# Hybrid decoder step on one core: store queue, T's DRAM tile, a gate buffer and a filler's order in the mixer

## The chip, the cores and the metric

The kernel runs on one core of a Trainium2 chip. The metric is the device time of one execution in microseconds (us). A core has a matrix engine (PE, TensorE), three engines for elementwise work (DVE, ACT and POOL), and a sequencer without arithmetic (SP). SP, ACT and POOL also issue DMAs, each from its own queue and in program order: an instruction that waits holds back everything behind it on its engine.

## The reference

One layer of a decoder trunk for a prompt of 1024 tokens and 8 samples of 4 tokens: a gated feed-forward block, a mixer, and a second feed-forward block, each with a conditioned norm and a residual. The mixer has two branches that share an input and an output projection:

```
xb, gb, pr = h @ w_in                       # RG-LRU input, RG-LRU gate, RWKV rows
# RG-LRU: convolution of 4 taps, two gates, a linear recurrence, then the output gate
y_lru  = linear_scan(a, b, h0) * gelu(gb)
# RWKV-7, a head: state S [value, key], a token at a time
S = S * w_t + (S @ a_t) b_t^T + v_t k_t^T ;  y_t = S @ r_t
y_rwkv = (group_norm(y) + bonus) * g
out = concat(y_lru, y_rwkv) @ w_out
```

## The kernel before, in words

The program goes feed-forward, mixer, feed-forward. A float32 product is done as three matmuls on rounded parts (lines 61 to 63). The order of the instructions on each engine is settled when the program is built: a scheduler with a timeline of its own sorts what the code emits, and the code's generators say what may be mixed.

The mixer (about 940 to 1465 us) has two stages that matter here.

**Preparation.** For each of four pairs of heads there are steps for the projections, for token-major rows, and for the inverse T of the triangular matrix of each chunk of 64 tokens. `prep_v` turns three matrices into token-major rows: PE transposes a block into PSUM (`ptr`), ACT copies it to a buffer `kbv` (two buffers; blocks 0 to 3 share one, 4 to 7 the next, and the samples' block 8 is small), and DMAs store it in DRAM: six stores of 128 KB to `dC` after block 3 and six after block 7, and one of 48 KB to `dKs` after block 8. Between these steps stand those of the RG-LRU: convolution input (`lru_x`), gates and scan (`lru_g`), and output gate (`lru_e`: a gelu on ACT of the projection, written to a buffer called "D", then a product on DVE). T's blocks are written by `inverse` and `merge` into columns of `dC` and read back by `merge` (`iX`).

**Chain.** `chain` runs over 16 chunks. `load(c)` fetches the rows of a chunk from `dC` into `ch` (64 rows for each of two halves) and `X2`, two chunks ahead, from ACT's queue. Then a chunk is a sequence that goes back and forth: matmuls `pw` from `ch`, ACT copies them to `W`, matmuls `pu` multiply W by T, ACT and DVE copy them to `X2`, matmuls `pd` update the state, DVE adds (`St`, `ch` of the next chunk, lines 956 and 960). The output of two chunks goes through a group norm (`yc`, `gva`) and a transpose `ptY`. While this sequence waits for other engines, PE runs a filler, a generator that yields a step at a time: the samples' recurrence (`sample_rwkv`), the second half of the RG-LRU (`lru(2, 4)`), then the output projection w_out (`po`). In `sample_rwkv` the output rows are gathered by 8 DMAs of 8 KB into `y2`; what follows (`gated`) has DVE instructions that write `late` (lines 1003 and 1009).

Weights come in blocks `wr` of 512 KB by DMAs from SP's queue, one buffer, and ACT and DVE split each into two parts (`wh`, `wl`, lines 46 and 47). DMAs that SP and ACT issue share eight semaphores in turn, so an issue also waits until the DMA before it on the same semaphore has landed.

Of the kernel before, what the change touches and what calls it, by code (L numbers as in the profile page):

```python
# [8 lines left out]
F32 = mybir.dt.float32  # L9
# [5 lines left out]
D, NP, NB, TS = 1024, 1024, 8, 4  # L15
# [14 lines left out]
CL = 64  # L30
# [8 lines left out]
def trunk(tc, a):  # L39
    nc = tc.nc  # L40
    es = ExitStack()
    const = es.enter_context(tc.tile_pool(name="const", bufs=1, reuse_waits="tile"))
    PL_, m = {"wn": T}, {}
# [472 lines left out]
    dram = es.enter_context(tc.tile_pool(name="dram", bufs=1, space=bass.MemoryType.DRAM))  # L516


    RW = 2304
    dC = [dram.tile([NP, RW], F32, name=f"dc{h}") for h in range(2)]  # L520
    MN = (256, 0)
    OV = (0, 2048)
    O2, OT, OG = 1024, 1536, 1792
    dKs = dram.tile([2, 2, 32, 2, 192], F32, name="dks")
    dM = dram.tile([4, NC, 128, 64], F32, name="dm")
    dGs = dram.tile([2, 2, 32, 2, 128], F32, name="dgs")
# [245 lines left out]
    def prep_v(hp_, kt, bt, Pp, Ps, rk, bv):  # L772
        D_ = nc.gpsimd.dma_start
        v_ = shifted(8 + hp_, 16 + hp_)
        for ci, (c, n) in enumerate(CH):
            ps = Q([128, n], "pbo")
            nc.tensor.matmul(ps, rk, bv[:, c:c + n], start=True, stop=True)
            nc.vector.tensor_tensor(bv[:, c:c + n], ps, v_[:, c:c + n], op=ALU.mult)
        for par in range(2):
            D_(dBV[hp_ % 2, :, hp_ // 2, par], bv[64 * par:64 * par + 64])  # L780

        for s in range(9):
            n = 128 if s < 8 else 32
            pt = Q([128, 3, 128], "ptr")
            for j, src in enumerate((kt, bt, v_)):
                nc.tensor.transpose(pt[0:n, j, :], src[:, 128 * s:128 * s + n], ident)
            if s % 4 == 0:
                kb = PL_['sm_'].tile([128, 4, 2, 3, 64], F32, tag="kbv", name="kbv")
            nc.scalar.activation(kb[0:n, s % 4].rearrange("p a j v -> p j a v"), pt[0:n].rearrange("p j (a v) -> p j a v", a=2), AF.Copy)
            if s == 8:  # L790
                nc.scalar.dma_start(dKs[:, hp_ % 2, :, hp_ // 2].rearrange("a t f -> t a f"), kb[0:32, 0].rearrange("p a j v -> p a (j v)"))
            elif s % 4 == 3:
                for par in range(2):
                    o2 = O2 + 64 * (4 * par + hp_)
                    for j, h, off in ((0, 1 - par, MN[1 - par] + o2), (1, par, MN[par] + o2), (2, 1 - par, OV[1 - par] + 64 * hp_)):
                        nc.scalar.dma_start(dC[h][128 * (s - 3):128 * (s + 1), off:off + 64].rearrange("(b r) f -> r b f", r=128), kb[:, :, par, j])

    def trow(par, g, s0, t0):
        off = MN[par] + OT + 64 * g + t0
        return dC[par][:, off:off + 32].rearrange("(c s) t -> c s t", s=CL)[:, s0:s0 + 32]  # L800

# [94 lines left out]
    def chain(fill):  # L898
# [2 lines left out]

        def load(c):

            ch = PL_['rg'].tile([128, 2560], F32, tag="ch", name="ch")
            X2 = PL_['rg'].tile([128, 8, 64], F32, tag="X2", name="X2")
            for h in range(2):
                r = slice(64 * h, 64 * h + 64)
                nc.scalar.dma_start(ch[r, 256 * h:256 * h + RW], dC[h][CL * c:CL * c + CL])
                nc.scalar.dma_start(X2[r, 4 - 4 * h:8 - 4 * h].rearrange("p g v -> p (g v)"), dC[h][CL * c:CL * c + CL, OV[h]:OV[h] + 256])
            x1 = lambda par: ch[:, 0:256].rearrange("p (g v) -> p g v", g=4) if par else ch[:, 2304:2560].rearrange("p (g v) -> p g v", g=4)  # L910
            v4 = lambda o, n: ch[:, 256 + o:256 + o + n].rearrange("p (g t) -> p g t", t=64)
            return x1, X2, ch[:, 256:1280].rearrange("p (h j t) -> p h j t", h=8, j=2), v4(O2, 512), v4(OT, 256), v4(OG, 256)

        late, wait, FN = None, 0, CFG["fn"]

# [119 lines left out]
    def sample_rwkv(late):  # L1035
# [73 lines left out]
        for g2 in range(2):  # L1109
            es_ = tp.rearrange("p (j b v) -> p j b v", j=2, b=NB)  # L1110
            for j in range(2):
                src = kb[:, g2, 128:192] if j == 0 else U[:, g2]
                nc.vector.tensor_tensor(es_[:, j], src.unsqueeze(1).to_broadcast([128, NB, 64]), bm, op=ALU.mult)
            yield
            for l in range(2):
                update(g2, l, es_)
                yield
            nc.sync.dma_start(a["s_wkv"][:, 2 * g2:2 * g2 + 2], S0[g2])
            if g2 == 0:
                pt = MM([128, 128], "ptS")  # L1120
                nc.tensor.transpose(pt, yc[:, 0:2].rearrange("p a b -> p (a b)"), ident)
                ys = o([128, 128], F32, "ys")
                nc.scalar.activation(ys, pt, AF.Copy)
                y2 = o([128, 4, 32], F32, "y2")
                for h2_ in range(2):
                    for g1 in range(2):
                        for par in range(2):
                            q = 32 * (2 * par + g1)
                            nc.gpsimd.dma_start(y2[64 * g1:64 * g1 + 64, 2 * h2_ + par], ys[64 * h2_:64 * h2_ + 64, q:q + 32])
        sx.close()  # L1130
        yield
        gated(NP, 32, lambda j: y2[:, j].unsqueeze(1), o, "mm")
        yield

# [15 lines left out]
    def LR(s, n=T):  # L1150
        return LRT[0][:, LRT[1][s]:LRT[1][s] + n]
# [47 lines left out]
        nc.vector.tensor_copy(m["hO"][:, f, 0:1], gx[:, NP - 1:NP])  # L1199
        nc.vector.tensor_copy(m["hO"][:, f, 1:9].unsqueeze(2), smp(gx[:, NP:T])[:, :, 3:4])  # L1200

    def lru_e(f):
        h, ge = LR("C"), LR("D")
        for p in half_proj(4 + f):
            if p:
                ci, c, n, ps = p
                nc.scalar.activation(ge[:, c:c + n], ps, AF.Gelu_apprx_tanh)
                if f == 3:
                    nc.vector.tensor_tensor(h[:, c:c + n], h[:, c:c + n], ge[:, c:c + n], op=ALU.mult)
            yield  # L1210
        if f < 3:
            nc.vector.tensor_tensor(h, h, ge, op=ALU.mult)
            nc.gpsimd.dma_start(dY[f], h)

    def lru(f0, f1):
        yield from lru_x(f0)
        lru_conv(f0)
        for f in range(f0, f1):
            if f < f1 - 1:
                yield from lru_x(f + 1)  # L1220
            yield from lru_g(f)
            if f < f1 - 1:
                lru_conv(f + 1)
            yield from lru_e(f)

    def w_load(half, og):
        return [weight(a["w_out"][4 * half + 2 * j:4 * half + 2 * j + 2, :, 512 * og:512 * og + 512].rearrange("k p o -> p k o")) for j in range(2)]
# [352 lines left out]
    with ExitStack() as ph:  # L1580
# [28 lines left out]
        def filler():  # L1609
            s_, l_ = sample_rwkv(late), lru(CFG["order"].count("X"), 4)  # L1610
            next(s_)
            yield

            for used in range(CFG["pre"]):
                next(l_)
                yield
            used = CFG["pre"]
            for i, _ in enumerate(s_):
                yield
                for _ in range(CFG["mix"] if i >= CFG["st"] else 0):  # L1620
                    if used < 12:
                        used += 1
                        next(l_)
                        yield
            yield from l_
            wo = w_out()
            next(wo)
            to_y()
            yield from wo
# [125 lines left out]
```

## Time and profile before

| | before |
|---|---|
| median of 3 runs | 2238.94 us (2236.42 to 2241.89) |
| the profiled execution | 2240.2 us |
| its span, first to last instruction | 2238.4 us |
| mean granted PE clock | 0.972 |
| PE busy | 2113.9 us, 94% |
| DVE busy | 1409.3 us, 63% |
| ACT busy | 734.1 us, 33% |

The span is what the profile's clock of microseconds runs over; 1.8 us of the execution lie outside it. Busy time counts what an engine computes; waits on DMAs, and the issuing of DMAs, are not counted. The granted clock is PE's, 1.00 at 2.4 GHz and 0.50 at 1.2 GHz.

### The profile page before, as it was taken

To read this page: it belongs to the slowest core of one execution; us is meant where nothing else is said; L and a number is where in the kernel's file an instruction comes from. 1 tells how busy PE (TensorE), PEld (TensorE's weight loads), DVE (VectorE), ACT (ScalarE), POOL (GpSimd) and SP (SyncE) were. 2 spreads that over 40 slices of the span, in tenths; PEclk is the share of its full clock that TensorE was granted. 3 is DMA by queue.
4 is the path that set the end of the run, shared out by engine and by line. 5 is a ranking of instruction groups with operands and counts; after the bars stand their busy time and mean duration, and the time that the engine had idled before them with its cause. 6 is when DMAs were issued, how large, how long until landed. Compare 5 with 4: busy or idle time off the path is not lost.

```text
span 2238.4 us, 41844 instructions
## 1 busy us (share of the span) xinstructions
PE 2113.9 (94%) x17209; PEld 2000.5 (89%) x17209; DVE 1409.3 (63%) x2954; ACT 734.1 (33%) x1283; POOL 212.2 (9%) x314
## 2 busy tenths in 40 slices
PE   6899999999999999999887889979999999999997
PEld 4899999999999988888886668878999999999997
DVE  5755555565956566674844676578666666585655
ACT  5533232323312144343333251246333333331213
POOL 0000000000000041214220100100000000100004
PEclk9999999999999999999898999989999999999998
DMA  6244444443723121446476756441222222262312
GB/s 249 86 147 145 141 152 138 138 146 110 234 84 103 51 99 42 97 106 150 112 161 157 184 149 152 146 145 57 73 82 82 75 75 86 92 216 87 100 44 78
DMA packets 145662, 266.80 MB, mean 119 GB/s; under 512 B 75504, under 2 KB 90048, under 8 KB 143424
## 3 DMA queue, kind: packets, MB, share of 16 engines
q1 hardware_dynamic: 76672, 165.51, 23.5%
q0 software_dynamic: 19312, 63.18, 9.0%
q10 hardware_dynamic: 49488, 35.45, 7.0%
q8 instruction: 135, 2.21, 0.4%
q14 instruction: 55, 0.45, 0.1%
HBM read 200.20 MB, written 63.82 MB: 118 GB/s over the span
## 4 chain that ended last, share of the span: by engine, by line
PE 74%; DVE 9%; DMA 5%; issue 4%; ACT 4%; ACTq 1%; POOL 1%; DVEq 0%; POOLq 0%
PE pd L61 7%; PE pd L62 7%; PE pd L63 7%; PE pX L61 4%; PE pZ L61 4%; PE pX L62 3%; PE pZ L63 3%; PE pX L63 3%; PE pW L61 3%; PE pW L63 3%; PE pW L62 3%; PE pZ L62 3%; PE pY L63 2%; PE pY L61 2%; PE pY L62 2%
## 5 line engine op out<-in xcount | busy, mean ns | idle before, releaser
L61 PE MATMUL pd<-fl,wh 128*128 128x384 f32 (+1 forms) x1056 | 340.6, 325 | 3.2 <-DVE fl L47 2.6
L63 PE MATMUL pd<-fh,wh 128*128 128x384 f32 (+1 forms) x1056 | 341.6, 324 | 0.0
L62 PE MATMUL pd<-fh,wl 128*128 128x384 f32 (+1 forms) x1056 | 341.5, 324 | 0.0
L46 ACT ACTIVATE wh<-wr 128x512 fp32r<-128x512 f32 (+1 forms) x254 | 192.3, 761 | 249.9 <-PE pZ L63 71.7
L47 DVE TENSOR_TENSOR wl<-wr,wh 128x512 fp32r<-128x512 f32 (+1 forms) x254 | 215.1, 851 | 87.5 <-ACT wh L46 82.1
L61 PEld LDWEIGHTS pd<-fl,wh 128*128 128x128 f32 x1056 | 198.5, 189 | 4.9 <-ACT wh L46 2.7
L62 PEld LDWEIGHTS pd<-fh,wl 128*128 128x128 f32 x1056 | 199.7, 189 | 0.0
L63 PEld LDWEIGHTS pd<-fh,wh 128*128 128x128 f32 x1056 | 199.4, 189 | 0.0
L61 PE MATMUL pW<-t,wh 128*128 128x266 f32 (+1 forms) x640 | 182.6, 285 | 0.0
L63 PE MATMUL pW<-t,wh 128*128 128x266 f32 (+1 forms) x640 | 182.3, 285 | 0.0
L62 PE MATMUL pW<-t,wl 128*128 128x266 f32 (+1 forms) x640 | 182.2, 285 | 0.0
L463 DVE SCALAR_TENSOR_TENSOR x<-pd,g3c,x 128x384 f32<-128x384 f32 (+1 forms) x192 | 107.1, 569 | 82.6 <-PE pd L63 82.6
L463 DVE SCALAR_TENSOR_TENSOR x<-pd,g1c,x 128x384 f32<-128x384 f32 (+1 forms) x192 | 107.8, 568 | 76.8 <-PE pd L63 76.6
L344 POOL DMA_DIRECT2D dh<-hf x88 | 48.0, 546 | 976.0 <-DVE hf L425 793.8
L419 ACT ACTIVATE e<-e,bt 128x262 f32<-128x262 f32 x80 | 41.3, 516 | 293.4 <-DVE bt L418 273.8
L46 ACT ACTIVATE fh<-wr 128x1056 fp32r<-128x1056 f32 x44 | 47.6, 1082 | 246.5 <-PE pd L63 195.9
L62 PEld LDWEIGHTS pW<-t,wl 128*128 128x128 f32 x640 | 120.8, 189 | 0.0
L61 PEld LDWEIGHTS pW<-t,wh 128*128 128x128 f32 x640 | 120.5, 188 | 0.0
L63 PEld LDWEIGHTS pW<-t,wh 128*128 128x128 f32 x640 | 120.5, 188 | 0.0
L47 DVE TENSOR_TENSOR wl<-s,wh 128x512 fp32r<-128x512 f32 x120 | 82.7, 690 | 58.5 <-ACT wh L46 58.5
L416 DVE TENSOR_TENSOR e<-pZ,e 128x266 f32<-128x266 f32 x80 | 34.5, 431 | 104.3 <-PE pZ L63 104.1
L46 ACT ACTIVATE wh<-s 128x512 fp32r<-128x512 f32 x120 | 75.4, 629 | 68.4 <-PE pW L63 31.4
(496 smaller groups left out, 5908.5 us busy)
## 6 DMA issues: line engine op xcount, KB each, us to landing
wa<-in_w_ada SPq DMA_DIRECT2D x72, 512.0 KB, 4.0
dh<-hf POOLq DMA_DIRECT2D x88, 264.0 KB, 2.3
wr<-dh SPq DMA_DIRECT2D x44, 528.0 KB, 4.3
wr<-in_ffn_w_gate SPq DMA_DIRECT2D x44, 512.0 KB, 3.5
wr<-in_ffn_w_up SPq DMA_DIRECT2D x44, 512.0 KB, 3.5
wr<-in_ffn_w_down SPq DMA_DIRECT2D x44, 512.0 KB, 3.9
ch<-dc ACTq DMA_DIRECT2D x32, 576.0 KB, 7.2
wr<-in_w_in SPq DMA_DIRECT2D x22, 512.0 KB, 4.0
```

Source lines behind the costliest of these rows:

```text
L46: nc.scalar.activation(hi, raw, AF.Copy)
L47: nc.vector.tensor_tensor(lo, raw, hi.bitcast(F32), op=ALU.subtract)
L61: nc.tensor.matmul(ps, wh, xl, start=(first and i == 0), stop=False, **kw)
L62: nc.tensor.matmul(ps, wl, xh, start=False, stop=False, **kw)
L63: nc.tensor.matmul(ps, wh, xh, start=False, stop=(last and i == n - 1), **kw)
L344: nc.gpsimd.dma_start(self.dH[m][:, 528 * p:528 * p + 528], hf)
L416: tt(g2, pz, u, op=ALU.add)
L419: nc.scalar.activation(g2[:, 0:n], g2[:, 0:n], AF.Silu, bias=bt[:, 0:1])
L463: nc.vector.scalar_tensor_tensor(x[:, ob, c:c + np_], ps[:, 0:np_], g[:, ob, 0:1], x[:, ob, c:c + np_], op0=ALU.mult, op1=ALU.add)
```

## The change

Five edits, all in the mixer:

1. The stores of `prep_v` are issued from SP's queue and not from ACT's, and block 8 comes first and not last.
2. T has DRAM tiles of its own, `dTT[0]` and `dTT[1]` (256 columns); the rows of `dC` shrink from 2304 to 2048 columns. `load(c)` has two more DMAs of 64 KB a chunk (`tt`), issued from ACT's queue.
3. Of the 8 DMAs that gather `y2`, four are issued from SP's queue; all eight were on POOL's.
4. `lru_e` writes the gelu of the last feature block of each half to buffer "A", of the others to "D" as before.
5. The filler leaves `sample_rwkv` at the gather for eight steps of the RG-LRU, and then does the samples' gated output.

```diff
-    RW = 2304
+    RW = 2048
     dC = [dram.tile([NP, RW], F32, name=f"dc{h}") for h in range(2)]
...
-    OV = (0, 2048)
-    O2, OT, OG = 1024, 1536, 1792
+    OV = (0, 1792)
+    O2, OG = 1024, 1536
+    dTT = [dram.tile([NP, 256], F32, name=f"dtt{h}") for h in range(2)]
...
-        for s in range(9):
+        for s in (8, *range(8)):
...
-                nc.scalar.dma_start(dKs[:, hp_ % 2, :, hp_ // 2].rearrange("a t f -> t a f"), kb[0:32, 0].rearrange("p a j v -> p a (j v)"))
+                nc.sync.dma_start(dKs[:, hp_ % 2, :, hp_ // 2].rearrange("a t f -> t a f"), kb[0:32, 0].rearrange("p a j v -> p a (j v)"))
...
-                        nc.scalar.dma_start(dC[h][128 * (s - 3):128 * (s + 1), off:off + 64].rearrange("(b r) f -> r b f", r=128), kb[:, :, par, j])
+                        nc.sync.dma_start(dC[h][128 * (s - 3):128 * (s + 1), off:off + 64].rearrange("(b r) f -> r b f", r=128), kb[:, :, par, j])
...
     def trow(par, g, s0, t0):
-        off = MN[par] + OT + 64 * g + t0
-        return dC[par][:, off:off + 32].rearrange("(c s) t -> c s t", s=CL)[:, s0:s0 + 32]
+        off = 64 * g + t0
+        return dTT[par][:, off:off + 32].rearrange("(c s) t -> c s t", s=CL)[:, s0:s0 + 32]
...
                 nc.scalar.dma_start(ch[r, 256 * h:256 * h + RW], dC[h][CL * c:CL * c + CL])
+                nc.scalar.dma_start(tt[r].rearrange("p g t -> p (g t)"), dTT[h][CL * c:CL * c + CL])
...
-                            nc.gpsimd.dma_start(y2[64 * g1:64 * g1 + 64, 2 * h2_ + par], ys[64 * h2_:64 * h2_ + 64, q:q + 32])
+                            (nc.gpsimd, nc.sync)[g1].dma_start(y2[64 * g1:64 * g1 + 64, 2 * h2_ + par], ys[64 * h2_:64 * h2_ + 64, q:q + 32])
         sx.close()
-        yield
+        yield "y2"
...
-    def lru_e(f):
-        h, ge = LR("C"), LR("D")
+    def lru_e(f, at="A"):
+        h, ge = LR("C"), LR(at)
...
-            yield from lru_e(f)
+            yield from lru_e(f, "D" if f < f1 - 1 else "A")
...
-            for i, _ in enumerate(s_):
+            for i, at in enumerate(s_):
                 yield
+                if at:
+                    break
...
+            for _ in range(8):
+                next(l_)
+                yield
+            for _ in s_:
+                yield
             yield from l_
```

The scheduler sorts the instructions anew, so their order shows more than the diff. The first place is ACT in the third `prep_v`, before:

```order
L789 ACTIVATE kbv<-ptr 128x3x2x64 x3
L796 DMA dc_82<-kbv 128x4x64
L796 DMA dc_81<-kbv 128x4x64
L796 DMA dc_82<-kbv 128x4x64
L796 DMA dc_81<-kbv 128x4x64
L796 DMA dc_82<-kbv 128x4x64
L796 DMA dc_81<-kbv 128x4x64
L789 ACTIVATE kbv<-ptr 32x3x2x64
L1207 ACTIVATE lr<-pj 128x384
L1207 ACTIVATE lr<-pj 128x288
```

and the same place of the change (`L1207` is `L1210` there):

```order
L790 ACTIVATE kbv<-ptr 32x3x2x64
L790 ACTIVATE kbv<-ptr 128x3x2x64
L1210 ACT_TABLE_LOAD
L1210 ACTIVATE lr<-pj 128x384
L790 ACTIVATE kbv<-ptr 128x3x2x64 x7
L1210 ACTIVATE lr<-pj 128x384
L1210 ACTIVATE lr<-pj 128x288
```

No DMA stands between the copies any more; the twelve stores stand on SP, between two loads of `wr`.

The second place is ACT where the chain begins. Before, the loads of chunks 0 and 1 stand in two groups:

```order
L909 DMA X_12739<-dc_81 64x256
L909 DMA X_12739<-dc_82 64x256
L909 DMA X_12747<-dc_81 64x256
L909 DMA X_12747<-dc_82 64x256
L869 ACTIVATE iX<-pa 32x512 x2
L615 ACTIVATE x<-pj 128x384
L908 DMA ch<-dc_81 64x2304 x2
L908 DMA ch<-dc_82 64x2304 x2
```

In the change eight loads stand ahead of the last copies `iX` of `merge`, and those of T come after the first `W` (rows of the change from the last of the eight on):

```order
L912 DMA X_12753<-dc_82 64x256
L870 ACTIVATE iX<-pa 32x512 x2
L616 ACTIVATE x<-pj 128x384 x2
L618 ACTIVATE x<-pj 128x256
L619 ACTIVATE x<-pj 128x8x4
L46 ACTIVATE wh<-wr 128x1024
L1176 ACTIVATE x<-x,vec 128x1024
L1176 ACTIVATE x<-x,vec 128x32
L942 ACTIVATE W<-pw 128x256
L911 DMA tt<-dtt_83 64x256 x2
L911 DMA tt<-dtt_84 64x256 x2
L947 ACTIVATE X_12742<-pu 64x256
```

The loads of `ch` no longer stand behind `merge`, and those of T stand behind `W` of chunk 0.

The third place is PE in the last chunk. Before, rows of w_out stand between its steps, for instance around `pu` (52 `po` in all between `pw` and `ptY`):

```order
L63 MATMUL po<-h1hy,wh 128x384
L61 MATMUL po<-h1ly,wh 128x384
L943 MATMUL pu<-W,ch 64x64 x8
L62 MATMUL po<-h1hy,wl 128x384
L63 MATMUL po<-h1hy,wh 128x384
```

In the change nothing stands between them:

```order
L970 MATMUL py<-ch 64x64 x7
L946 MATMUL pu<-W,tt 64x64 x8
L957 MATMUL pd<-X_14998,ch 64x64
L971 MATMUL py<-X_14998,ch 64x64
L957 MATMUL pd<-X_14998,ch 64x64 x7
L971 MATMUL py<-X_14998,ch 64x64 x7
L1028 MATMUL ptY<-ident,yc 128x128 x4
L1010 MATMUL pgt<-sgd,g2w 128x128 x4
L61 MATMUL po<-h2ly,wh 128x288
```

The rows of `po` that filled the last chunk stand in earlier chunks.

## Rows read from the trace of the kernel before

**Rows 1.** The page: engines' busy time, and the chain that ended last by engine.

```profile
PE 2113.9 (94%) x17209; PEld 2000.5 (89%) x17209; DVE 1409.3 (63%) x2954; ACT 734.1 (33%) x1283; POOL 212.2 (9%) x314
...
PE 74%; DVE 9%; DMA 5%; issue 4%; ACT 4%; ACTq 1%; POOL 1%; DVEq 0%; POOLq 0%
```

**Rows 2.** Stretches: length, busy time of each engine, clock, DMA share, GB/s.

```profile
1140.00:1160.00 20.00, 15.01 (x78) 14.40 (x78) 3.54 (x5) 4.10 (x9) 2.95 (x6) 0.83 0.90 192
...
1200.00:1220.00 20.00, 12.86 (x201) 10.76 (x203) 10.72 (x24) 1.53 (x4) 0.00 (x0) 0.74 0.74 160
...
1260.00:1280.00 20.00, 13.78 (x137) 10.54 (x137) 11.84 (x31) 5.99 (x10) 0.79 (x1) 0.83 0.79 220
...
1320.00:1340.00 20.00, 14.69 (x142) 13.37 (x141) 19.80 (x43) 11.09 (x25) 0.75 (x1) 0.91 0.56 139
1340.00:1360.00 20.00, 20.00 (x201) 17.90 (x198) 14.83 (x34) 4.17 (x8) 0.75 (x1) 1.00 0.71 190
```

**Rows 3.** PE's waits from 1140 to 1345 us: total, times, longest.

```profile
PE pw L937 <- DMA ch<-dc: 7.0, 1, 7.0
PE pw L937 <- issue: 5.9, 1, 5.9
PE pj L61 <- ACT lr L1207: 5.0, 1, 5.0
...
PE pu L943 <- ACT W L939: 2.6, 2, 2.1
...
PE po L61 <- ACT x L1207: 2.3, 1, 2.3
```

**Rows 4.** ACT's timeline from 1136 to 1167 us: start, duration, instruction, [idle before].

```profile
1136.23 9.27 ACTq L796 DMA_DIRECT2D dc<-kbv  x6
1145.55 1.25 ACT L789 ACTIVATE kbv<-ptr 128x384 f32<-128x384 f32 x3 [9.35 <-DMA dc<-kbv]
1146.83 5.12 ACTq L796 DMA_DIRECT2D dc<-kbv  x6
...
1152.44 0.46 ACT L1207 ACTIVATE lr<-pj 128x384 f32<-128x384 f32 x1
...
1166.28 1.06 ACT L46 ACTIVATE wh<-wr 128x1024 fp32r<-128x1024 f32 x1 [1.06 <-DMA wr<-in_w_in]
```

**Rows 5.** Stretches of 4 us behind the stalls, columns as in rows 2.

```profile
1152.00:1156.00 4.00, 3.04 (x9) 3.04 (x10) 2.77 (x3) 2.55 (x5) 0.58 (x1) 0.50 0.61 129
1156.00:1160.00 4.00, 4.00 (x20) 4.00 (x20) 0.77 (x3) 0.29 (x1) 0.00 (x0) 0.76 1.06 298
...
1332.00:1336.00 4.00, 4.00 (x16) 3.94 (x14) 3.94 (x12) 0.53 (x1) 0.75 (x1) 0.57 0.96 221
```

**Rows 6.** PE's timeline at chunk 0.

```profile
1196.00 2.27 PE L1069 MATMUL psS<-x 64*32 64x512 f32 x16
1205.31 1.12 PE L937 MATMUL pw<-ch 128*64 128x64 f32 x16 [7.04 <-DMA ch<-dc]
...
1207.21 1.12 PE L943 MATMUL pu<-W,ch 64*64 64x64 f32 x16
```

**Rows 7.** ACT's timeline at chunk 0.

```profile
1194.22 2.40 ACTq L908 DMA_DIRECT2D ch<-dc  x4
...
1206.47 0.39 ACT L939 ACTIVATE W<-pw 128x256 f32<-128x256 f32 x1 [6.58 <-PE pw L937]
```

**Rows 8.** DMA issues of the whole run: queue, count, KB each, median us to landing.

```profile
X<-dc ACTq DMA_DIRECT2D x32, 64.0 KB, 6.2
...
out_s_wkv<-x SPq DMA_DIRECT2D x2, 512.0 KB, 7.1
...
dc<-iX POOLq DMA_DIRECT2D x8, 64.0 KB, 3.0
...
x<-x POOLq DMA_DIRECT2D x8, 8.0 KB, 7.1
```

**Rows 9.** DVE's timeline at chunk 4.

```profile
1261.47 0.55 DVE L1003 SCALAR_TENSOR_TENSOR late<-x,vec 128x32 f32<-128x32 f32 x2 [3.07 <-DMA x<-x]
...
1265.67 0.42 DVE L956 TENSOR_TENSOR St<-pd,pc 128x256 f32<-128x256 f32 x1
```

**Rows 10.** PE's timeline at the last chunk.

```profile
1432.87 0.67 PE L968 MATMUL py<-X,ch 64*64 64x64 f32 x14
...
1438.59 0.66 PE L1025 MATMUL ptY<-ident,yc 128*128 128x128 f32 x4 [2.60 <-DVE yc L992]
```

More of the change, by code (lines that the diff above doesn't have):

```diff
@@ L902, in load @@
         def load(c):
-            ch = PL_['rg'].tile([128, 2560], F32, tag="ch", name="ch")
+            ch = PL_['rg'].tile([128, 2304], F32, tag="ch", name="ch")
+            tt = PL_['rg'].tile([128, 4, 64], F32, tag="tt", name="tt")
             X2 = PL_['rg'].tile([128, 8, 64], F32, tag="X2", name="X2")
@@ L908, in load @@
                 nc.scalar.dma_start(ch[r, 256 * h:256 * h + RW], dC[h][CL * c:CL * c + CL])
+                nc.scalar.dma_start(tt[r].rearrange("p g t -> p (g t)"), dTT[h][CL * c:CL * c + CL])
                 nc.scalar.dma_start(X2[r, 4 - 4 * h:8 - 4 * h].rearrange("p g v -> p (g v)"), dC[h][CL * c:CL * c + CL, OV[h]:OV[h] + 256])
-            x1 = lambda par: ch[:, 0:256].rearrange("p (g v) -> p g v", g=4) if par else ch[:, 2304:2560].rearrange("p (g v) -> p g v", g=4)
+            x1 = lambda par: ch[:, 0:256].rearrange("p (g v) -> p g v", g=4) if par else ch[:, 2048:2304].rearrange("p (g v) -> p g v", g=4)
             v4 = lambda o, n: ch[:, 256 + o:256 + o + n].rearrange("p (g t) -> p g t", t=64)
-            return x1, X2, ch[:, 256:1280].rearrange("p (h j t) -> p h j t", h=8, j=2), v4(O2, 512), v4(OT, 256), v4(OG, 256)
+            return x1, X2, ch[:, 256:1280].rearrange("p (h j t) -> p h j t", h=8, j=2), v4(O2, 512), tt, v4(OG, 256)
         late, wait, FN = None, 0, CFG["fn"]
```

## The prediction

> **What bounds the kernel now.** I begin with the page: PE is busy 94% of the span, no other engine above 63%, and PE makes up 74% of the chain that ended last [rows 1]. So PE's work is the floor, and the change leaves that work as it is. It can only move the times at which PE stands idle, and those at which it runs at a lower clock. The table of stretches says where these are: from 1340 us on PE is busy all the time at clock 1.00, but in four stretches before it is busy 12.9 to 15.0 us of 20 at 0.74 to 0.91 [rows 2]. PE's waits over the same time give each hole its name [rows 3]: 7.0 us for the first chunk's `ch`, 5.9 us at a `pw` that waits for nothing the profile shows, 5.0 us for a gelu on ACT, 2.3 us for another gelu and up to 2.1 us for `W`. What counts is whether each of these goes, and where else PE then waits.
>
> A hole costs more than its length, because the clock is at 0.50 behind it: in the 4 us after the 5.0 us hole PE is busy 3.04 us at 0.50, in the next 4 us at 0.76 [rows 5]. At full clock that work would take 3.04 x 0.50 and 4.00 x 0.76 us, so 1.5 + 1.0 = 2.5 us are lost. Behind the 2.3 us hole a stretch is at 0.57, which loses 4.00 x 0.43 = 1.7 us.
>
> **Stores on SP (edit 1).** In the third `prep_v` ACT spends 9.27 us on issuing six stores, copies, spends 5.12 us on six more, and only then comes to the gelu for which PE waits [rows 4]. In the changed order the copies stand back to back with the gelu right behind. Full gain: 5.0 of idle time and 2.5 of clock, 7.5 us. Against it stands what the stores are moved past: SP carries the weights, and twelve stores plus the small one stand between two loads of `wr`. They are to be issued while PE works on a block that is already split. But ACT already waited 1.06 us for a `wr` soon after [rows 4], so some of the gain may come back there. I take -6.5, with bounds -8 (a little in the other `prep_v` too, where PE hardly waits) and 0 (all of it goes into late weights).
>
> The Trainium skill (DMA: Bandwidth & Descriptors, Issuing engines are not separate DMA queues) speaks against this edit: all queues feed the same 16 DMA engines, and issuing from several saves only the sequencer's time to start a DMA, usually small against the DMA itself. The trace agrees on what is saved, but here the issuing takes 14.4 us for twelve DMAs [rows 4], and PE waits behind it. By the rule this term would be nearly 0 and the sum +1.5; by the rows it is -6.5.
>
> **T in its own tile (edit 2).** PE ends the work before chunk 0 at about 1198.3 us and gets `ch` 7 us later [rows 6]. Before, the four loads of `ch` were issued at 1194.22 and take 0.6 us each [rows 7], behind the stores of `merge` that share their tile. After, they stand ahead of `merge`'s last copies, so `pw` can start at about 1198.3. But `pu` needs T, whose loads now stand on ACT behind `W`: `pw` 1.12 and `W` 0.39 [rows 6, 7] give 1199.8. The third of four issues completes chunk 0's halves, so add 3 x 0.6: 1201.6. A 64 KB transfer lands in 3.0 us (`dc<-iX`) to 6.2 us (`X<-dc`) [rows 8], so `pu` starts between 1204.6 and 1207.8, where it started at 1207.21 before. The same queue and direction is `X<-dc`, so I stay near it: -1, bounds -3 and +1. The 7 us hole would thus not go, but move from `pw` to `pu`, and its slow clock with it. If T were early, all of it would go: -7 and some clock. The other 28 loads of T cost ACT 0.6 us each, some 17 us over the 140 us after chunk 0's start. ACT is 33% busy [rows 1], so I set this at 0, and +2 if its queue is late for some `W`.
>
> **Gather and filler (edits 3 and 5).** At chunk 4 the DVE stands at `late` until the gather lands (3.07 us at 1261.47), more of `late` follows, and only at 1265.67 does it reach `St`, on which the next `pw` depends [rows 9]. That is the 5.9 us hole. The filler moves the samples' gated output back, but in the changed order the first instructions on `late` still stand on DVE ahead of `St` and `ch`; only the second ones (those with `pgt`) move. The gather itself lands after 7.1 us [rows 8], which issuing it from two queues shortens by at most its own issue time. On the other hand the RG-LRU's gates now stand on PE in front of chunk 4's `pw` and `pd`. The matmuls need a PSUM buffer that a tanh on ACT frees, and these tanh write a buffer that the stores `out_s_wkv` still read (7.1 us to landing [rows 8]). One hole goes and one of much the same length comes. I take +1, with bounds -6 (the hole goes) and +6 (both are there).
>
> **Gate buffer (edit 4).** Before, the last gelu writes the buffer the scan still reads. After, it follows the square root directly on ACT. The 2.3 us hole and its 1.7 us of clock go: -4.0; the 2.1 us for `W` a little later [rows 3] may go or not. I take -3.5, bounds -6 and 0.
>
> **The tail.** This loss isn't in the diff. In the last chunk 52 matmuls of w_out stood between `pw` and `ptY`; in the changed order none do, because they are used up earlier. From the end of `py` at 1433.54 to `ptY` at 1438.59 are 5.05 us, of which PE idled 2.60 [rows 10]. Uncovered, all 5.05 are idle: +2.45. The copies between `pw`, `pu` and `pd` are uncovered too, by the rows of chunk 0 some 0.4 us for `W` [rows 7] and twice that for `X2`: +1.2. A hole of 5 us was followed by some 2.5 us of lost clock above; here I take about half: +1.3. Together +5, bounds +3 and +6.5.
>
> **Sum.** -6.5 - 1 + 1 - 3.5 + 5 = -5.0 us. The profiled execution, 2240.2 us (span 2238.4 and 1.8 around it), would take 2235.2. It is 1.3 us above the median of 2238.9, so on the median the forecast is 2234 us. Differences under 0.2%, 4.5 us, are about what can't be told from no change.
>
> **Rivals.**
>
> *The stores only move the wait.* SP's queue holds the weights behind stores, and PE waits for `wr` where it waited for ACT. For it: the 1.06 us wait, and the skill's rule. Against it: SP's loads are mostly waiting for a free buffer, not for issue. The first term becomes 0: +1.5, 2240 us, no change.
>
> *Slower: the RG-LRU's gates block chunk 4.* The tanh wait for both `out_s_wkv`, one issued behind the other, and `pw` and `pd` stand behind them on PE. It decides if the second store lands after DVE is through with `late`. Then chunk 4 has two holes: +6 for that term, and with the slow clock behind the second, as above, 2.5 more. With the tail the sum is -6.5 - 1 + 8.5 - 3.5 + 5 = +2.5, and with T at its late bound (+2 against my value) and the gelu saving only its 2.3 us of idle time (+1.2) +5.7: 2245 us. For it: the order on PE. Against it: the first tanh may not be needed so soon.
>
> *All holes go.* T lands before `W` is there (-7 and 2.5 of clock) and the hole at chunk 4 closes (-6): -6.5 - 9.5 - 6 - 3.5 + 5 = -20.5, or about -13 if only one of the two: 2218 to 2226 us. Against it stand the places of T's loads on ACT and of `late` on DVE.
>
> **How the numbers follow.** The forecast case has 0.50, the moved wait 0.15, the slower one 0.20, all holes 0.15. The forecast's own range is -10 to 0, 2229 to 2239, a little over half of it beyond 0.2%. Faster: 0.29 + 0.15 + 0.02 from the moved wait = 0.46. Slower: 0.18 + 0.04 = 0.22. The same: 0.32. For 8 in 10 the range goes from the middle of the case of all holes, 2221, to the slower rival's 2246.
>
> **What would show it.** Right: no hole at the gelu near 1148 us; the wait at chunk 0 named for T at `pu`; a wait of `pw` or a gate matmul at chunk 4; no wait on a gelu near 1330 us; a `ptY` that waits about 5 us at the chain's end. Wrong: PE waiting for `wr` between 1150 and 1185 us, T landed before `W`, `St` of chunk 4 not behind `late`, or a tail no longer than before. The largest single error would be chunk 0 or chunk 4, where a hole may go or double.

## The result, and the profile after

The changed kernel takes 2211.37 us (median of 4 runs, 2204.8 to 2214.32), the kernel before on the same chip 2240.41 us (4 runs, 2236.42 to 2243.1). The ratio is 0.9861, 95% interval 0.9844 to 0.9878: 29 us between the medians, 1.4% by the ratio. The forecast of 2234 us had the right sign and a sixth of the size, and the time lies below its range. The profiled execution of the changed kernel is the fastest of the four: 2204.8 us, span 2203.0. The lengths of stages below are those of the two profiled executions and differ by 35.4 us in sum, 6 us more than the medians. The page after, against [rows 1]:

```profile
PE 2098.9 (95%) x17209; PEld 1989.5 (90%) x17209; DVE 1409.2 (64%) x2954; ACT 743.2 (34%) x1289; POOL 209.4 (10%) x310
...
PE 76%; DVE 10%; DMA 3%; issue 3%; ACT 3%; POOL 1%; SPq 1%; ACTq 0%; DVEq 0%; POOLq 0%
```

PE executes the same 17209 matmuls, and its busy time falls by 15 us. Busy time contains what a lower clock adds to each matmul, so idle time and clock have both to be counted. The three rows below are whole stages of the kernel before (length, busy time of each engine, clock, DMA share, GB/s): the preparation, from the first `pj` to the first `pw` of chunk 0; the chain, to the last `ptY`; the end of the mixer, to the first gate matmul of the second feed-forward block.

```profile
824.06:1205.31 381.25, 351.55 (x3439) 318.24 (x3437) 237.48 (x561) 144.64 (x241) 90.84 (x134) 0.95 0.50 118
1205.31:1438.59 233.28, 208.38 (x2125) 174.88 (x2125) 151.79 (x328) 64.06 (x116) 13.32 (x21) 0.94 0.59 148
1438.59:1480.32 41.73, 29.97 (x228) 29.28 (x229) 26.97 (x67) 14.79 (x26) 3.98 (x6) 0.94 0.59 192
```

The same stages of the changed kernel:

```profile
820.42:1174.22 353.80, 334.60 (x3421) 305.28 (x3421) 232.64 (x555) 149.68 (x244) 90.23 (x134) 0.98 0.53 126
1174.22:1401.84 227.62, 210.61 (x2141) 176.49 (x2142) 155.58 (x336) 68.66 (x120) 14.35 (x20) 0.93 0.61 158
1401.84:1444.88 43.04, 33.23 (x228) 32.70 (x228) 27.45 (x67) 14.65 (x26) 0.86 (x1) 0.82 0.46 161
```

The preparation is 27.4 us shorter, the chain 5.7 us shorter, the end 1.3 us longer; 3.6 us come before the mixer, where the code is unchanged, and nothing after it. (The mixer's first `pj` stands at 824 us, so the mixer begins before the 940 us given above.) Length minus busy time is idle time: 29.7 against 19.2 us in the preparation. The rest is split with rows of 2 us: busy time times (1 - clock) is lost to the clock, busy time times clock is work at full clock, each summed over the stage.

| us | preparation: idle, clock, work | chain: idle, clock, work |
|---|---|---|
| before | 29.7, 17.4, 334.1 | 24.9, 11.9, 196.5 |
| after | 19.2, 3.7, 331.0 | 17.0, 13.6, 197.0 |

Work stays the same to 1%; 13.7 of the 27.4 us of the preparation come out of the clock. The prediction had looked only at holes named in [rows 3], from 1140 us on. PE's waits from 824 us on have one more of that size in the kernel before, near 1078 us, and the changed kernel has it no longer:

```profile
PE pgl L1183 <- DVE edge L636: 3.6, 1, 3.6
```

Stretches of 20 us (columns as in [rows 2]) show the missing place, in the kernel before:

```profile
1060.00:1080.00 20.00, 16.38 (x93) 14.03 (x92) 9.90 (x19) 10.68 (x18) 0.58 (x1) 0.73 0.24 69
1080.00:1100.00 20.00, 20.00 (x294) 17.59 (x294) 18.22 (x36) 8.73 (x12) 6.21 (x9) 0.93 0.67 151
1100.00:1120.00 20.00, 17.54 (x223) 16.98 (x221) 19.38 (x53) 2.03 (x3) 8.08 (x13) 0.83 0.49 112
```

and in the changed kernel, where everything from 1000 to 1160 us stands at clock 1.00 and the low clock comes later, at chunk 0, at chunk 4 and in the tail above all:

```profile
1060.00:1080.00 20.00, 18.21 (x230) 15.53 (x229) 18.58 (x29) 10.42 (x14) 3.76 (x5) 1.00 0.67 159
1080.00:1100.00 20.00, 19.09 (x307) 18.35 (x308) 19.31 (x57) 2.06 (x4) 10.85 (x17) 1.00 0.59 132
1100.00:1120.00 20.00, 19.38 (x128) 17.57 (x127) 17.47 (x52) 8.25 (x15) 8.41 (x14) 1.00 0.62 147
...
1160.00:1180.00 20.00, 14.34 (x117) 10.75 (x116) 7.51 (x14) 5.57 (x11) 2.07 (x3) 0.75 0.85 202
...
1220.00:1240.00 20.00, 16.05 (x141) 9.91 (x140) 10.16 (x23) 8.42 (x13) 1.12 (x3) 0.79 0.91 258
...
1400.00:1420.00 20.00, 15.56 (x90) 15.27 (x91) 14.44 (x33) 7.54 (x12) 0.64 (x1) 0.69 0.52 178
```

PE's waits of the changed kernel from 1130 to 1300 us, against [rows 3]:

```profile
PE pd L957 <- ACT X L947: 4.3, 3, 3.5
PE pws L880 <- ACT x L616: 3.3, 1, 3.3
...
PE pw L940 <- DVE wl L47: 2.3, 1, 2.3
...
PE pu L946 <- DMA tt<-dtt: 0.7, 1, 0.7
```

The gelu's 5.0 us are gone and no wait for `wr` took their place. ACT in the third `prep_v` shows why, against [rows 4]: the last copies and the gelu's step `lr` follow each other, with short waits for PE's transposes.

```profile
1116.42 0.87 ACT L790 ACTIVATE kbv<-ptr 128x384 f32<-128x384 f32 x2 [0.55 <-PE ptr L787]
1117.61 0.49 ACT L790 ACTIVATE kbv<-ptr 128x384 f32<-128x384 f32 x1 [0.31 <-PE ptr L787]
1118.00 0.49 ACT L1210 ACTIVATE lr<-pj 128x384 f32<-128x384 f32 x1
```

The twelve stores cost SP as much as they cost ACT, 4.98 and 8.92 us, and the next `wr` stands behind them. ACT waits for it (4.08 us at 1137.04), but PE does not stand idle for that:

```profile
1114.37 4.98 SPq L797 DMA_DIRECT2D dc<-kbv  x6
1119.44 2.60 SPq L847 DMA_DIRECT2D iM<-dm  x2
1122.15 8.92 SPq L797 DMA_DIRECT2D dc<-kbv  x6
1131.18 0.47 SPq L52 DMA_DIRECT2D wr<-in_w_in  x1
```

Chunk 0 went another way than forecast. ACT needs 9 us to issue the eight loads, and everything behind is late:

```profile
1160.43 0.50 ACTq L910 DMA_DIRECT2D ch<-dc  x1
...
1165.12 4.32 ACTq L912 DMA_DIRECT2D X<-dc  x2
1169.49 1.20 ACT L870 ACTIVATE iX<-pa 32x512 f32<-32x512 f32 x2 [9.09 <-DMA ch<-dc]
1170.71 0.87 ACT L616 ACTIVATE x<-pj 128x384 f32<-128x384 f32 x2
...
1171.81 1.08 ACT L46 ACTIVATE wh<-wr 128x1024 fp32r<-128x1024 f32 x1
```

On PE this gives two holes where [rows 6] have one, together 5.65 us in place of 7.04, and T is waited for by 0.66 us alone:

```profile
1171.25 0.65 PE L880 MATMUL pws<-x 32*32 32x64 f32 x16 [3.33 <-ACT x L616]
1174.22 1.12 PE L940 MATMUL pw<-ch 128*64 128x64 f32 x16 [2.32 <-DVE wl L47]
...
1180.89 0.68 PE L946 MATMUL pu<-W,tt 64*64 64x64 f32 x14 [0.66 <-DMA tt<-dtt]
```

The issue of a load waits for an earlier DMA on the same of the eight shared semaphores. The trace names the semaphore of each DMA (all those of SP and ACT use eight, those of POOL eight others), and so which hold this was: the first seven loads are out at 1165.72 us, after 5.3 us; the eighth stands until 1168.99, for 3.26 us, because its semaphore is that of a block of weights (`wr` from w_out) that SP issued at 1160.71 and that lands at 1168.97. The `ch` that the profile names as releaser in the row of `iX` isn't what the load waited for.

At chunk 4 the DVE stands at `late` as before [rows 9], but `St` is only 2.6 us behind the gather, not 4.2:

```profile
1224.17 0.57 DVE L1006 SCALAR_TENSOR_TENSOR late<-x,vec 128x32 f32<-128x32 f32 x2 [3.27 <-DMA x<-x]
...
1226.75 0.41 DVE L959 TENSOR_TENSOR St<-pd,pc 128x256 f32<-128x256 f32 x1
```

The single hole of 5.9 us becomes several of 0.4 to 1.1 us, 3.8 us in sum. In the tail, `ptY` waits 4.64 us in place of 2.60 [rows 10], because the rows of w_out are used up:

```profile
1401.84 1.12 PE L1028 MATMUL ptY<-ident,yc 128*128 128x128 f32 x4 [4.64 <-DVE yc L995]
```

### The profile page after: what moved, and what is told of

Same layout as the page of the kernel before. It is cut to its first block, busy times and chain, and to the rows that moved or that the text cites. A ratio compares the mean times of both kernels' runs of the same rounds, so it can differ in the third digit from the quotient of the medians.

```text
span 2203.0 us, 41916 instructions
## 1 busy us (share of the span) xinstructions
PE 2098.9 (95%) x17209; PEld 1989.5 (90%) x17209; DVE 1409.2 (64%) x2954; ACT 743.2 (34%) x1289; POOL 209.4 (10%) x310
## 4 chain that ended last, share of the span: by engine, by line
PE 76%; DVE 10%; DMA 3%; issue 3%; ACT 3%; POOL 1%; SPq 1%; ACTq 0%; DVEq 0%; POOLq 0%
PE pd L61 7%; PE pd L62 7%; PE pd L63 7%; PE pX L61 4%; PE pZ L61 4%; PE pX L62 4%; PE pZ L63 4%; PE pX L63 4%; PE pW L61 4%; PE pW L63 4%; PE pW L62 4%; PE pZ L62 4%; PE pY L63 2%; PE pY L61 2%; PE pY L62 2%
```

## The experiments

Theory A: the gain is the sum of the edits, each in its own stage, and the stores alone make most of it. Rival B: the edits act through each other, so that none alone gives its share. Rival C: the stores gain nothing by leaving ACT, and T's tile or the gate buffer makes the preparation shorter. All ratios are to the kernel before on the same chip (medians there 2240.4 to 2241.7 us), with a 95% interval; the lengths of the stages come from the profiled execution of each. Over all these executions the code before and behind the mixer, which is the same in all, varies by 4.5 and 5.0 us, so a difference of 2 or 3 us in one stage tells nothing. Each length is from one execution, and executions of the kernel before alone spread from 2233 to 2251 us, so one of 5 us tells little.

| kernel | ratio | preparation | chain |
|---|---|---|---|
| before | 1 | 381.2 | 233.3 |
| after | 0.9861 [0.9844, 0.9878] | 353.8 | 227.6 |
| only_stores | 0.9924 [0.9901, 0.9947] | 364.9 | 231.5 |
| only_t | 1.0025 [1.001, 1.004] | 378.8 | 242.6 |
| only_gate | 1.0004 [0.9988, 1.0019] | 373.6 | 241.5 |
| only_order | 1.0002 [0.9988, 1.0015] | 382.6 | 235.0 |
| no_stores | 0.9982 [0.9968, 0.9997] | 371.1 | 240.8 |
| no_t | 0.9924 [0.9898, 0.995] | 359.8 | 236.5 |
| no_gate | 0.9946 [0.9926, 0.9967] | 360.4 | 238.3 |
| no_order | 0.9898 [0.9876, 0.9919] | 355.4 | 234.4 |
| stores_p0 | 0.9993 [0.998, 1.0006] | 372.1 | 240.8 |
| stores_p1 | 0.9985 [0.997, 1.0001] | 376.6 | 230.6 |
| stores_p2 | 1.0004 [0.9989, 1.002] | 376.7 | 236.7 |
| stores_p3 | 0.9966 [0.9949, 0.9982] | 374.8 | 233.9 |
| stores_pool | 0.9976 [0.9962, 0.9991] | 359.8 | 251.4 |
| s8_last | 0.9894 [0.987, 0.9918] | 358.6 | 230.7 |
| loads_sp | 0.9899 [0.988, 0.9917] | 358.8 | 234.0 |
| c1_sp | 0.9869 [0.9837, 0.9901] | 355.4 | 227.8 |
| first_pool | 0.9982 [0.997, 0.9995] | 353.6 | 253.9 |
| gate_small | 0.9998 [0.9983, 1.0013] | 375.8 | 242.1 |

**One edit alone, or all but one.** `only_stores` is the kernel before with edit 1, `only_t` with edit 2, `only_gate` with edit 4, `only_order` with edits 3 and 5; `no_stores`, `no_t`, `no_gate` and `no_order` are the changed kernel without them. The lines are those of the diff above, for instance:

```diff
-                        nc.scalar.dma_start(dC[h][...], kb[:, :, par, j])
+                        nc.sync.dma_start(dC[h][...], kb[:, :, par, j])
```

> The kernel before with edit 1 alone (stores of prep_v from SP's queue, block 8 first). Theory S: the preparation's 26 us came from ACT no longer issuing the stores; then this run gains 18 to 24 us against the kernel before, its pw of chunk 0 starts 18 us or more earlier, and PE runs at clock 1.00 between 1040 and 1120 us. Theory T: the gain came from T leaving dC, since the loads iX no longer wait for kbv's stores (7.7 us on SP); then this run gains at most 8 us, the 5 us hole alone. Theory O: any new order of the preparation gives some of it; then 8 to 15 us.

> The kernel before with edit 2 alone (T in DRAM tiles of its own). Theory S: within 4 us of the kernel before; the 5 us hole in the third prep_v stays. Theory T: 12 to 20 us faster, with the waits of SP for kbv's stores gone and weights loaded earlier. Theory O: anywhere from 8 us slower to 10 us faster.

> The changed kernel with edit 1 undone (stores from ACT's queue, block 8 last). Theory S: it loses 18 to 24 us of the 29, so 5 to 11 us faster than the kernel before. Theory T: it keeps 20 us or more. Theory O: 10 to 18 us faster than before.

> The changed kernel with edit 2 undone (T in columns of dC, four loads a chunk). Theory S: 22 to 29 us faster than the kernel before. Theory T: at most 12 us faster, and SP's loads iX, with weights behind them, wait for kbv's stores. The wait at chunk 0 for ch should come back in either, 3 to 7 us.

> The kernel before with edit 4 alone (gelu of the last feature block of each half to buffer A). Theory: half of the RG-LRU stands in the preparation, so the edit also frees the gelu there; 3 to 6 us faster than the kernel before, from before chunk 0. The prediction's account (only the gelu near 1330 us): 2 to 4 us, all of it in the chain. Rival: nothing, as the hole at the gelu only moves.

> The changed kernel with edit 4 undone (all gelus to buffer D). Theory, parts add up in the preparation: it is 7 to 8 us longer, 360 to 363 us; the chain as in the changed kernel or up to 8 us longer by the gelu of the last block: 2217 to 2228 us. Rival, the gate's gain in the preparation was the wait that the stores made and is not there without them: 353 to 356 us, and 2209 to 2214 us.

> The kernel before with edits 3 and 5 alone. Theory: no change in the preparation, 380 us; in the chain a gain only where T and the gate have made it longer, so 230 to 236 us: 2236 to 2244 us. Rival: the order itself saves the hole at chunk 4 and more, the chain is 222 to 228 us: 2230 to 2235 us.

> The changed kernel with edits 3 and 5 undone (gather on POOL's queue alone, the samples' output right behind it). Theory: in the preparation the parts add up (stores 16, gate 8, T 2 us), in the chain they don't: T and the gate each lengthen it by 8 to 9 us alone, and the filler's order takes that away. Then the preparation stays at 352 to 357 us and the chain is 236 to 245 us, with idle time at chunk 4: 2220 to 2229 us. Rival: the order of the filler is worth nothing and the chain stays at 226 to 232 us: 2209 to 2216 us.

*Preparation.* Here the edits add: stores -16.3, gate -7.6, T -2.4, order +1.4, together -24.9 us against -27.4 for all. Taken out of the changed kernel they cost 17.3, 6.6, 6.0 and 1.6 us: about the same, but for T. So theory A holds in this stage, as far as single profiles tell, and rival C falls. The 16.3 us of the stores are 5.9 idle, 8.9 clock and 1.5 work (381.2 against 364.9: idle 23.8, clock 8.5, work 332.6). Of the gate's 7.6 us, 1.3 are idle and 7.8 clock (idle 28.4, clock 9.6, work 335.5), and PE's wait for the gelu in the third `prep_v` is still 4.8 us there.

*Chain.* Here they don't: stores -1.8, T +9.3, gate +8.2, order +1.7 would be +17.4, and all together give -5.7. So rival B holds in this stage. The order of the filler is worth nothing alone and some 8 us in company (0.9898 against 0.9861, with intervals that just touch); T alone makes the kernel slower and in company makes it faster (0.9924 against 0.9861).

One way in which a chain gets longer is that ACT is held while it issues loads. In `only_gate` its queue shows a load of `X` that goes out only when a transfer of another engine's queue has landed:

```profile
1314.49 0.69 ACTq L908 DMA_DIRECT2D ch<-dc  x1
1326.36 0.45 ACTq L909 DMA_DIRECT2D X<-dc  x1
1326.86 0.63 ACT L987 ACTIVATE ysq<-yc 128x512 f32<-128x512 f32 x1 [14.30 <-DMA x<-dx]
1327.39 0.36 ACT L939 ACTIVATE W<-pw 128x256 f32<-128x256 f32 x1
```

The transfer `x<-dx` is the second of two on SP's queue:

```profile
1310.64 2.93 SPq L1313 DMA_DIRECT2D x<-dx  x2
```

It has 768 KB and the semaphore of the load of `X`. SP issues it at 1313.21 us, it lands at 1326.34, and the load goes out at 1326.36, held for 11.18 us. PE, which needs `W` from ACT, stands still:

```profile
1327.81 1.12 PE L943 MATMUL pu<-W,ch 64*64 64x64 f32 x16 [7.93 <-ACT W L939]
```

A slow transfer of SP's thus stops ACT, and ACT stops PE, though the transfer has no data for either of them. By the semaphores, the holds of over 4 us of ACT's loads by an earlier DMA on the same semaphore are, in the chain: 11.18 us in `only_gate` and 12.18 in `gate_small` (behind `x<-dx`), 10.34 in `stores_pool` (a load of `tt` behind SP's weights), 5.08 in `no_order`, 4.27 in `stores_p2`, and 4.27 in `no_stores` (a load of `X` behind a gather of 8 KB that edit 3 moved to SP, which took 10.0 us to land). There is none in the kernel before and none in the changed kernel. For `only_gate` the rows show the whole path. But `only_t`, `no_gate`, `stores_p0` and `first_pool` have long chains without such a hold, so it is one cause and not the account of all; in `only_t` and `no_gate` what makes the chain longer stays unexplained.

In `no_gate` a part of the rival named "slower" came true, which it didn't in the changed kernel: the first tanh of the gates waits for the samples' state to be stored. PE's gate matmul then waits for ACT by 1.32 us only, behind a wait of 3.64 us for DVE.

```profile
1239.70 1.28 ACT L1187 ACT_TABLE_LOAD   x1 [6.90 <-DMA out_s_wkv<-x]
```

**One pair's stores on SP.** In the kernel before, only pair K of `prep_v` gets edit 1 (`stores_p0` to `stores_p3`):

```diff
-        for s in range(9):
+        for s in ((8, *range(8)) if hp_ == K else range(9)):
...
-                        nc.scalar.dma_start(dC[h][...
+                        (nc.sync if hp_ == K else nc.scalar).dma_start(dC[h][...
```

> The kernel before with the stores of the first prep_v alone (pair 0, about 965 to 977 us) from SP's queue, its block 8 first. Theory, the pairs add up: pairs 0 and 3 make up 7 us of the preparation together, so 2 to 5 us here (376 to 379 us), and the slow stretch from 1060 us may be gone. Rival, only all together: 380 to 383 us here, and the slow stretch is there.

> The kernel before with the stores of the second prep_v alone (pair 1, about 1045 to 1059 us) from SP's queue, its block 8 first. Theory S (ACT's issuing also delayed the copies that the second prep_v's neighbours need, and the slow clock from 1060 to 1112 us and the 3.6 us hole at 1078 us come from that): 6 to 12 us faster than the kernel before, with the hole in the third prep_v still there. Rival, that of the prediction (PE hardly waits there): 0 to 2 us.

> The kernel before with the stores of the third prep_v alone (pair 2, about 1133 to 1153 us) from SP's queue, its block 8 first. The prediction's term: 6.5 us faster (5.0 of idle time and 2.5 of clock, less 1.0). If weights behind the stores take it back: 0 to 3 us. If the two prep_v need each other: under 4 us here and under 4 us in the run with pair 1.

> The kernel before with the stores of the fourth prep_v alone (pair 3, about 1170 to 1183 us) from SP's queue, its block 8 first. Theory, the pairs add up: 2 to 5 us of the preparation (376 to 379 us), all of it after 1170 us. Rival, only all together: 380 to 383 us.

Each pair shortens the preparation: -9.1, -4.6, -4.5 and -6.4 us. The gain isn't that of the one pair with the gelu, as the prediction had it; moved alone, that pair (`stores_p2`) leaves the time as it was. In sum it would be -24.6, more than the -16.3 of all four: a hole or a slow stretch that one edit takes away can't be taken away again. Three of the four change the time by nothing that can be told. In `stores_p0` and `stores_p2` the chain is longer by 7.5 and 3.4 us; for `stores_p1` the profiled execution is 3 us below the median of its runs.

There is a rival that these four runs don't exclude. Each edit makes the scheduler sort the whole preparation anew. In `stores_p0` and `stores_p1` PE waits for the gelu of the third `prep_v` by 0.7 and 0.9 us in place of 5.0, although that pair's stores still stand on ACT (6.70 and 6.76 us of issuing in `stores_p1`, where two of the gelu's three steps now stand ahead of the last six stores). A hole behind a busy queue can thus go by a change of order alone, and what one pair's queue is worth can't be read from one pair's run. That it counts to free ACT of all stores rests on three comparisons of kernels with the stores on ACT and on another queue, in which the preparation is 16.3 us shorter (`only_stores`), 17.3 (`no_stores` against the changed kernel) and 11.3 (`no_stores` against `stores_pool`, below).

**Which queue, and which block first.** `stores_pool` issues the stores of the changed kernel from POOL; `s8_last` leaves them on SP with block 8 last.

```diff
-                        nc.sync.dma_start(dC[h][...
+                        nc.gpsimd.dma_start(dC[h][...
```

```diff
-        for s in (8, *range(8)):
+        for s in range(9):
```

> The changed kernel with the stores of prep_v issued from POOL's queue in place of SP's. Theory A (what counts is that ACT doesn't issue them): the preparation stays at 352 to 358 us where with stores on ACT it was 371. Rival B (SP is what counts, since the loads iX and weights stand behind the stores in one order): 362 to 372 us, as POOL's stores of the inverse, T and bonus stand behind.

> The changed kernel with block 8 last in prep_v as before, stores on SP. Theory A (ACT free is all): the preparation within 3 us of 353.8 us and the run at 0.985 to 0.988 of the kernel before. Rival C (block 8 first frees the buffers kbv earlier, and part of the 16 us is that): 358 to 365 us and 0.989 to 0.993.

From POOL the preparation is 359.8 us, although it ends with a wait of 7.28 us for `ch` at chunk 0 (5.65 after); with the stores on ACT it is 371.1. So it's ACT's freedom that counts, not SP. The chain is then 24 us longer, and its first hole follows at once, behind the hold of 10.34 us named above:

```profile
1182.73 1.12 PE L940 MATMUL pw<-ch 128*64 128x64 f32 x16 [7.28 <-DMA ch<-dc]
1191.50 1.12 PE L946 MATMUL pu<-W,tt 64*64 64x64 f32 x16 [6.80 <-ACT W L942]
```

Block 8 first is worth 4.8 us in the preparation and 0.3% of the time, with intervals that overlap a little (0.9894 against 0.9861).

**The loads at chunk 0.** If the hold of ACT by its own loads costs the holes at chunk 0, loads from elsewhere should close them. `loads_sp` issues all loads of all chunks from SP, `first_pool` those of chunks 0 and 1 from POOL, `c1_sp` those of chunk 1 from SP:

```diff
-                nc.scalar.dma_start(ch[r, ...
+                (nc.sync if c == 1 else nc.scalar).dma_start(ch[r, ...
```

> The changed kernel with all loads of the chain (ch, tt, X2) issued from SP's queue and not from ACT's. Theory Q (what is left at chunk 0, 3.3 us at pws and 2.3 us at pw, comes from ACT being held 9 us by eight loads, and the chain's copies W and X2 are late for the same reason): 5 to 10 us faster than the changed kernel, 1.5% to 1.8% faster than the kernel before, with no wait for ACT's L616 before chunk 0. Rival: the loads wait on SP behind a load of weights that waits for its buffer (13.8 us at 1160.7); then ch is late for chunk 0 and the run is the same or slower than the changed kernel.

> The changed kernel with the loads of chunks 0 and 1 alone (ch, tt, X2) issued from POOL's queue, the others from ACT's. Theory Q (ACT held 9 us by eight loads in front of merge's copies makes the 3.3 and 2.3 us at chunk 0): both go, ch and T land later or not at all later, 3 to 6 us faster than the changed kernel, ratio 0.983 to 0.985 to the kernel before. Rival: the wait for ch comes back at pw of chunk 0 (5.6 us in the run with all loads on SP), and the run is the same as the changed kernel or slower, 0.986 to 0.989.

> The changed kernel with the loads of chunk 1 (and of no other) issued from SP's queue. ACT then issues four loads in front of merge's copies in place of eight, and T's loads for chunk 0 stand before W. Theory Q: ACT is held under 4 us in place of 9; the waits of 3.3 us (pws, for ACT) and 2.3 us (pw) go or are under 2 us together; 3 to 6 us faster than the changed kernel, 0.983 to 0.985. Rival: ch of chunk 0 lands no earlier and PE waits for it as long: 0.985 to 0.988.

None is faster than the changed kernel. In `c1_sp` ACT issues four loads, and is held at the fourth all the same, by 4.46 us: its semaphore is again that of SP's `wr` from w_out, which lands at 1169.77 us.

```profile
1169.79 0.45 ACTq L912 DMA_DIRECT2D X<-dc  x1
1170.29 1.20 ACT L870 ACTIVATE iX<-pa 32x512 f32<-32x512 f32 x2 [7.21 <-DMA X<-dc]
```

In `first_pool` ACT is free, and PE waits for `ch` and `tt` themselves; later in this kernel a gate matmul stands 7.02 us behind a tanh that waits for `out_s_wkv`:

```profile
1175.30 0.69 PE L940 MATMUL pw<-ch 128*64 128x64 f32 x16 [4.16 <-DMA ch<-dc]
1181.95 0.45 PE L946 MATMUL pu<-W,tt 64*64 64x64 f32 x2 [3.55 <-DMA tt<-dtt]
...
1242.36 1.33 PE L1186 MATMUL pgl<-x,lru_wa 128*128 128x288 f32 x2 [7.02 <-ACT x L1187]
```

In `loads_sp` PE waits 5.55 us for `ch`, and in `c1_sp` it waits 1.7 us each at `pws` and `pw` and 2.7 us for `tt`. Some 5 to 8 us at chunk 0 thus stay whoever issues. That this is the time in which the last pair's rows reach DRAM and come back is argued, not shown.

**A smaller store.** `gate_small` is `only_gate` with less to store from the buffers that the tanh writes; it leaves out most of the samples' state output.

```diff
-nc.sync.dma_start(a["s_wkv"][:, 2 * g2:2 * g2 + 2], S0[g2])
+nc.sync.dma_start(a["s_wkv"][:, 2 * g2:2 * g2 + 1, 0:1], S0[g2][:, 0:1, 0:1])
```

> The kernel before with edit 4 alone, and of the samples' state only one sixteenth is stored (the rest of that output is left out). With edit 4 alone the chain was 241.5 us, and a tanh waited 6.2 us for that store. Theory W (the wait for the store makes the chain longer): 232 to 236 us, no tanh that waits for the store over 1 us. Rival O (the new order makes it): 238 to 242 us.

The chain stays at 242.1 us, as long as that of `only_gate`. But this doesn't settle what the store is worth: with 32 KB in place of 512 the second store still takes 9.6 us to land (11.0 in `only_gate`), and the tanh waits 8.1 us for it (6.2 there). The wait that the edit was to take away is still there, so neither expectation was put to the test. What the run does show is that the hold is not a chance of one execution: at the same place, near 1329 us, the load of `X` is held for 12.18 us by `x<-dx`, and PE's `pu` waits 8.71 us behind it.

## Why the prediction was wrong

**The bound and the sign** were right: PE's work is constant (334.1 and 331.0 us, 196.5 and 197.0), and only idle time and clock moved.

**Stores on SP: the step that failed.** The mechanism was right in kind: ACT's queue was blocked by issuing, and PE behind it. For the third pair the rows show it; for the others the experiments show the gain, and the path from the queue to PE isn't followed. The size was -6.5 and is -16.3 in the preparation (ratio 0.9924 alone, some 17 us). The failing sentence is the bound "a little in the other `prep_v` too, where PE hardly waits". Moved alone, the third pair leaves the time as it was (1.0004, -4.5 us in the preparation), and so most of the gain of all four comes with the others. The step took PE's waits after 1140 us for the whole, while the rows of the stretches from 1060 to 1120 us showed clocks of 0.73, 0.93 and 0.83; at those clocks and busy times they cost 16.38 x 0.27 + 20.00 x 0.07 + 17.54 x 0.17 = 8.8 us, besides 6.1 us idle, 3.6 of them the wait for `edge`. None of it had a term. Within them, one row is full of work at half clock, and another follows two waits of 0.90 and 1.56 us that no list of large waits would bring up (stretches of 4 us, kernel before):

```profile
1064.00:1068.00 4.00, 4.00 (x21) 3.97 (x21) 1.81 (x3) 2.37 (x3) 0.00 (x0) 0.50 0.21 85
...
1104.00:1108.00 4.00, 4.00 (x22) 3.94 (x18) 3.79 (x12) 0.00 (x0) 2.45 (x4) 0.50 0.47 109
```

Which pair's stores let the clock fall at 1064 us isn't settled: in `stores_p1` the same 4 us still have 0.51, in `stores_p2` 0.57, in `only_gate` 1.00 (with 0.57 only behind a hole at 1068), and in `only_stores` all from 1056 to 1080 us is at 1.00.

**The rule of the Trainium skill** (DMA: Bandwidth & Descriptors, Issuing engines are not separate DMA queues) said that another queue saves only the sequencer's time, usually small. The mechanism agrees, since SP spends 13.9 us where ACT spent 14.4. The measurement decides against "small" here, where ACT also feeds PE: moving this time off ACT made the kernel some 17 us shorter.

**Gate buffer.** The term counted one gelu near 1330 us, at -3.5. But the edited helper runs for both halves of the RG-LRU, and the first half stands in the preparation: -7.6 us there, nearly all of it clock; by which path isn't shown. Near 1330 us the named hole went, but a hole of 3.51 us at `pd` (behind ACT's `X`) came. Alone the edit is worth nothing (1.0004), since its chain gets 8.2 us longer.

**T in its own tile.** "`pu` starts between 1204.6 and 1207.8" rested on T as the last thing to come. It came almost in time (0.66 us); late was ACT, which needs 9.09 us for its eight loads, and its copies behind them, for which PE waits 3.33 us. The prediction counted 0.6 us for an issue, 4.8 for eight, and knew that issues wait for a semaphore, but gave that wait no price; 3.26 us is its size here. (Its 17 us for the other loads of T also stand over too short a time: the chain lasts 233 us and not 140.) The term -1 was near the -2.4 us of the preparation by luck.

**Gather and filler.** `late` still stands in front of `St`, as forecast, and the gates didn't block chunk 4; the hole shrank from 5.9 to 3.8 us. The term +1 fits the edit alone (1.0002) but not its 8 us in company.

**The tail** was right in kind. The stretch from the last chunk's first `pw` to `ptY` is 8.88 us in place of 15.71, and the 52 `po` that left it are worth about 52 x 0.173 = 9.0 us by the spacing of matmuls of that shape: +2.2; the end is 1.3 us longer: +3.5 in place of +5.

**The sum.** Alone, the four parts measure about -17, +6, +1 and 0 us: -10. Together they give -31 by the ratio. By the stages the missing 20 us are in the chain, so that better sizes would not have been enough: the prediction's sum assumes that the terms add, and there they don't. Of the rivals, "all holes go" came nearest (2218 to 2226), for another reason: the holes at chunks 0 and 4 remain in part. The range's ends, 2221 and 2246, are each a microsecond off the cases that they are taken from (2222 and 2245), which changes nothing.

What stays open: what lengthens each variant's chain but those of `only_gate` and `gate_small`, and so why all edits together avoid it; and how much of each small gain in the preparation is the new order of instructions and not the edit's own effect.

## What to carry to other kernels

Account for a stage as work at full clock, idle time and clock loss before pricing a change; the first is constant, and the list of large waits shows only part of the other two. Look for all places where an edited helper runs, not only for that with the largest wait. Where several queues take their semaphores from one rotation, an edit that adds or moves DMAs shifts who waits for whom; single-edit gains need not add there, and a part that loses alone may win in company: test it by taking it out of the whole as well. A releaser that a profile names is inferred: at chunk 0 it named `ch`, and the semaphore of the held load was that of a block of weights. And an experiment that is to take a wait away counts only if its trace no longer has the wait.

## What the runs showed of the hardware that was not expected

The granted clock was at 0.50 in two stretches of 4 us in which PE was busy for all 4.00 us (1064 to 1072 us in the kernel before; the 18 small matmuls `st` took 3.61 us there and 2.00 us at clock 1.00 in the changed kernel), and not only behind holes: from 1040 to 1060 us PE had been busy 19.75 of 20 us at 1.00. And two loads that follow each other on ACT's queue were issued 0.6 us apart in some places and 11.9 us apart in another (1314.49 and 1326.36 us in `only_gate`), by what another queue had under way. A store of 32 KB took nearly as long to land as one of 512 KB at the same place (9.6 us in `gate_small`, 11.0 in `only_gate`).
